# A trunk layer on one core: order of the products at each seam, x loads, first norm, last norm

## The chip, the core and the metric

The kernel runs on one core of a Trainium2 chip. TensorE (PE) multiplies, with its weight loads (PEld) beside it; VectorE (DVE), ScalarE (ACT) and GpSimd (POOL) work on tiles; SyncE (SP) and POOL issue the transfers. Every engine takes its instructions in the order in which they stand in its own queue, so one that waits holds up all behind it. The metric is the device time of one execution in microseconds. Before the change it was 1810.94 us, the median of 3 runs (1808.47 to 1815.28).

## What is computed

One decoder layer for 256 tokens of 2048 values in float32: half-step FFN, a mixer of two kinds of heads, half-step FFN, final norm.

```python
x = x + 0.5 * swiglu(rmsnorm(x, ffn1_norm), ffn1_w_gate, ffn1_w_up, ffn1_w_down)
h = rmsnorm(x, mix_norm)
a_q, a_k, a_v, m_q, m_k, m_v, m_o, m_i, m_f = split(h @ w_in)
x = x + concatenate([y_a, y_b]) @ w_out        # differential attention, mLSTM
x = x + 0.5 * swiglu(rmsnorm(x, ffn2_norm), ffn2_w_gate, ffn2_w_up, ffn2_w_down)
return rmsnorm(x, final_norm)
```

The hidden width is 5632, so the six FFN matrices, 46 MB each, make up most of what is read.

## The kernel before

**Three matmuls for one product.** Every float32 operand is split into a high and a low part: ACT casts the high part (`wh`, `xs`, `xt`; L115 or L110), DVE subtracts it from the source (`wl` and the like; L116 or L111). PE then makes high by high, high by low and low by high (L145, L146, L148), each 128x512. All matmuls run on such parts, so a weight tile always goes load, ACT, DVE, PE.

**Paired chunks.** Columns are done in chunks of 512, with two accumulators, one for each half of the tokens. `Paired` takes two column chunks (gate and up, or two chunks of a down projection) and, for the first `ns` pairs of row tiles, saves one product in eight by sums of blocks. Its `first()` loads a pair of both weights (`raw`, 2 x 512 KB), DVE forms `sums` (L376) and overwrites one block (L378), and after the splits PE makes P5 and P7 from the sums and then P1 and P6 from `raw`. Behind them the POOL queue adds one block of `raw` onto another by a transfer (L385). `combine()` stands at the seam to the next stage: ACT copies P1 to `u1` (L392), DVE adds P6 to it as `u2` (L393) and adds `u2` to P7 (L394), ACT copies that to `u3` (L395), and DVE forms the right chunk's accumulators (L396, L397). 44 such seams run. `second()` finishes the left chunk in P1 and P7: `bare(j)` with the blocks of `raw` that the POOL transfer has summed, `upper` for a third accumulator, and `plain` for the pairs that were not saved. `third()` finishes the right chunk; it is a stream that is woven into the next `first()`. There are six banks for accumulators and two (`ps_tr`) for transposes, and four `wh` and `wl` buffers.

**Stages.** FFN1 does its 11 hidden chunks in parts of 3, 3, 3 and 2. After each part come two paired down projections (c=0 and c=2); those of the first three parts have `ns`=3 and add their results into the residual `xres` through `part` (L286) and a POOL transfer (L287). Then come the mixer, `w_out` and FFN2 in the same way. A finished hidden chunk is transposed on PE (`hid_transposes`, L301, tile `hg`), a finished chunk of `xres` by `chunk_to_xt` (L248, tile `xg`); both are put on the list `pending`, from which `flush` takes them, and their splits and block sums (`xsum`, L278 to L280) run on ACT and DVE.

**Start and end.** `load_xt` loads the transposed x in 8 units of 256 KB (`xraw`, L553) among the first gate weights; `xres` (L566, 1 MB for each half of the tokens) is issued with a lower priority. `rstd1` squares `xres` in eight pieces (L235), and the row factor `rstd` is a power on POOL (L230), needed by the gate's Silu (`sg`, L314). At the end `store` does the last norm for one half of the tokens after the last column chunk.

**What sets the order.** A scheduler places each engine's instructions by priority: `tc.high_priority(offset=AHEAD)` moves work 400 steps forward (weight loads and splits), `soon()` 440 steps (`combine`, copies of transposes), the rest stands at its place in the program.

## Time and profile before

| | |
|---|---|
| Median of 3 runs | 1810.94 us |
| Profiled execution, and its span | 1805.68 us, 1803.9 us |
| DVE, ACT and POOL busy | 1571.9 us (87%), 1170.5 us (65%), 174.1 us (10%) |
| Transfers | 402.75 MB, mean 223 GB/s |
| Granted clock | 0.999 |

All times inside the execution count from the start of the span. A row of the timeline has the start, the length, the engine, the line, the operation with its tiles (out<-in) and, in brackets, how long the engine had stood idle before it and what released it. "SPq" is the moment at which SP issues a transfer, and not the transfer. PE's matmuls overlap, so a PE row's length is more than the step from one to the next.

### The profile page before, as it was taken

The numbers are of one execution on the slowest core, as the hardware profiler recorded it, in microseconds if no ns is written. First come the engines' busy times: TensorE is split into PE (matmuls) and PEld (weight loads), VectorE is DVE, ScalarE is ACT, GpSimd is POOL, SyncE is SP. The second block draws the span as 40 slices with busy tenths as digits, with TensorE's granted clock in tenths as the row PEclk, the third lists the DMA queues.
The fourth block names the chain that finished last, engine by engine and source line by source line (L and its number), as shares of the span: only waits on it lengthen the run. The fifth ranks groups of instructions, "written<-read, shape, count | busy, mean of one in ns | idle before, by whom it ended". The sixth has DMA issues, their size and how long they took to land.

```text
span 1803.9 us, 23316 instructions
## 1 busy us (share of the span) xinstructions
PE 1777.9 (99%) x8033; PEld 1461.1 (81%) x8033; DVE 1571.9 (87%) x1889; ACT 1170.5 (65%) x1523; POOL 174.1 (10%) x218
## 2 busy tenths in 40 slices
PE   9999999999999999999999999999999999999998
PEld 6788788888787887987888888788788878888886
DVE  6988889988998988797787988899889988998986
ACT  6666666666666666676565766666666666666664
POOL 0001100111002100000001000101100021002100
PEclk9999999999999999999999999999999999999999
DMA  8677887787778974676656666777887788678954
GB/s 339 216 216 231 226 253 222 241 242 229 218 240 246 271 234 126 214 227 184 190 185 210 182 190 180 218 232 228 230 243 234 239 239 246 210 241 249 267 188 152
DMA packets 125255, 402.75 MB, mean 223 GB/s; under 512 B 14160, under 2 KB 14160, under 8 KB 124880
## 3 DMA queue, kind: packets, MB, share of 16 engines
q1 hardware_dynamic: 96624, 349.28, 56.3%
q0 software_dynamic: 27216, 49.56, 16.2%
q10 hardware_dynamic: 1296, 2.42, 0.4%
q8 instruction: 63, 1.03, 0.2%
q14 instruction: 56, 0.46, 0.1%
HBM read 349.56 MB, written 2.10 MB: 195 GB/s over the span
## 4 chain that ended last, share of the span: by engine, by line
PE 85%; DMA 4%; DVE 3%; issue 2%; ACT 1%; POOL 1%; SPq 0%; POOLq 0%; DVEq 0%; ACTq 0%
PE acc L145 27%; PE acc L146 27%; PE acc L148 27%; DMA raw<-raw 3%; DVE wl L116 2%; PE tr L301 1%; ACT wh L115 0%; DMA raw<-in_wd_dram 0%; POOL xres L287 0%; PE sc L895 0%; POOL raw L385 0%; PE tr L248 0%; PE num L846 0%; DVE sums L376 0%; DVE acc L394 0%
## 5 line engine op out<-in xcount | busy, mean ns | idle before, releaser
L115 ACT CAST wh<-raw 128x1024 fp32r<-128x1024 f32 (+3 forms) x448 | 400.8, 907 | 245.1 <-PE acc L146 202.4
L145 PE MATMUL acc<-wh,xt 128*128 128x512 f32 (+2 forms) x1392 | 539.5, 389 | 1.4 <-ACT wh L115 0.8
L146 PE MATMUL acc<-wh,xt 128*128 128x512 f32 (+2 forms) x1392 | 538.4, 388 | 0.8 <-DVE xt L111 0.8
L116 DVE TENSOR_TENSOR wl<-raw,wh 128x1024 fp32r<-128x1024 f32 (+3 forms) x448 | 460.3, 1040 | 56.2 <-ACT wh L115 50.4
L116 DVE TENSOR_TENSOR wl<-rawp,wh 128x1024 fp32r<-128x1024 f32 (+1 forms) x358 | 431.7, 1209 | 69.3 <-ACT wh L115 57.6
L115 ACT CAST wh<-rawp 128x1024 fp32r<-128x1024 f32 (+1 forms) x358 | 372.7, 1043 | 154.4 <-PE acc L146 133.3
L145 PE MATMUL acc<-wh,xs 128*128 128x512 f32 (+2 forms) x1123 | 441.5, 396 | 10.3 <-ACT u L395 5.8
L146 PE MATMUL acc<-wh,xs 128*128 128x512 f32 (+2 forms) x1123 | 434.4, 389 | 0.5 <-DVE xs L111 0.5
L148 PE MATMUL acc<-wl,xt 128*128 128x512 f32 (+2 forms) x1392 | 388.1, 388 | 1.4 <-DVE wl L116 1.4
L148 PE MATMUL acc<-wl,xs 128*128 128x512 f32 (+2 forms) x1123 | 347.6, 387 | 0.1
L145 PEld LDWEIGHTS acc<-wh,xt 128*128 128x128 f32 x1392 | 261.2, 188 | 55.5 <-ACT xt L110 1.4
L146 PEld LDWEIGHTS acc<-wh,xt 128*128 128x128 f32 x1392 | 261.5, 188 | 54.1 <-DVE xt L111 1.6
L148 PEld LDWEIGHTS acc<-wl,xt 128*128 128x128 f32 x1392 | 260.0, 188 | 55.4 <-DVE wl L116 3.1
L145 PEld LDWEIGHTS acc<-wh,xs 128*128 128x128 f32 x1123 | 211.4, 188 | 62.8 <-ACT u L395 11.0
L385 POOL DMA_DIRECT2D raw<-raw x141 | 120.0, 851 | 1379.2 <-DVE wl L116 1137.2
L146 PEld LDWEIGHTS acc<-wh,xs 128*128 128x128 f32 x1123 | 211.6, 189 | 41.5 <-DVE xs L111 1.7
L148 PEld LDWEIGHTS acc<-wl,xs 128*128 128x128 f32 x1123 | 209.7, 188 | 43.6 <-DVE wl L116 1.0
L115 ACT CAST wh<-sums 128x1024 fp32r<-128x1024 f32 x141 | 148.6, 1054 | 113.6 <-PE acc L146 103.8
L376 DVE TENSOR_TENSOR sums<-raw 128x1024 f32<-128x1024 f32 x141 | 172.4, 1223 | 54.3 <-DMA raw<-in_wu_dram 28.3
L116 DVE TENSOR_TENSOR wl<-sums,wh 128x1024 fp32r<-128x1024 f32 x141 | 172.0, 1220 | 15.1 <-ACT wh L115 14.9
L378 DVE TENSOR_TENSOR raw<-sums,raw 128x512 f32<-128x512 f32 x141 | 96.5, 685 | 0.3
L287 POOL DMA_DIRECT2D xres<-part x48 | 45.5, 1169 | 96.0 <-ACT part L286 96.0
(191 smaller groups left out, 809.7 us busy)
## 6 DMA issues: line engine op xcount, KB each, us to landing
rawp<-in_wd_dram SPq DMA_DIRECT2D x96, 512.0 KB, 6.2
rawp<-in_wu_dram SPq DMA_DIRECT2D x94, 512.0 KB, 6.4
raw<-in_wg_dram SPq DMA_DIRECT2D x89, 512.0 KB, 7.0
rawp<-in_wg_dram SPq DMA_DIRECT2D x86, 512.0 KB, 5.3
raw<-in_wu_dram SPq DMA_DIRECT2D x82, 512.0 KB, 7.7
raw<-in_wd_dram SPq DMA_DIRECT2D x80, 512.0 KB, 6.4
raw<-raw POOLq DMA_DIRECT2D x141, 256.0 KB, 5.7
rawp<-in_win_dram SPq DMA_DIRECT2D x50, 512.0 KB, 4.6
```

The lines of the kernel that those rows point to most:

```text
L115: nc.scalar.copy(hi, src)
L116: nc.vector.tensor_tensor(out=lo, in0=src, in1=hi.bitcast(F32), op=ALU.subtract)
L145: nc.tensor.matmul(acc, lh, rh, start=first, stop=False, skip_group_check=on)
L146: nc.tensor.matmul(acc, ll, rh, start=False, stop=False, skip_group_check=on)
L148: nc.tensor.matmul(acc, lh, rl, start=False, stop=last, skip_group_check=on)
L287: nc.gpsimd.dma_start(xres[:, hb, c * CW:(c + 1) * CW], t, accum_op=ALU.add)
L301: nc.tensor.transpose(tr[:, i, hb * P:(hb + 1) * P], hs[hb][:, k * P:(k + 1) * P], ident)
L376: nc.vector.tensor_tensor(out=sums, in0=raw[:, 0:4:3, :], in1=raw[:, 2:3, :].to_broadcast([P, 2, CW]), op=ALU.add)
L378: nc.vector.tensor_tensor(out=raw[:, 2, :], in0=sums[:, 0, :], in1=raw[:, 3, :], op=ALU.add)
L385: nc.gpsimd.dma_start(raw[:, 2, :], raw[:, 1, :], accum_op=ALU.add)
```

## The change

At the last saved pair of each `first()` the order is now P1, P6, P7, P5, with the split of `raw` ahead of that of `sums`; the pairs before it keep P5, P7, P1, P6. `combine` works in one tile `u` in place of `u1` and `u2`. The transposes go on the list one by one (`run(j)`), and their splits have the priority of weight splits. The copies `sg` and `part` get `soon()`. The mixer's input gets three saved pairs, not four. At the start, x comes in two loads of 256 KB and three of 512 KB, the Silu table is loaded first, one block sum of x is made inside `load_xt`, and `rstd1` squares each half of the tokens in one instruction. Two small loads move from ACT's queue to POOL's. The last norm runs in two column halves of the last chunk, and the output leaves in pieces of 544 and 480 columns.

```diff
--- before.py
+++ after.py
...
+CUTS = ((0, 544, 0), (1088, 1568, 1), (544, 1088, 0), (1568, 2048, 1))
...
-    nc.scalar.copy(touch[:, 0:1], touch[:, 1:2])
+    nc.scalar.activation(touch[:, 0:1], touch[:, 1:2], AF.Silu)
...
     def chunk_to_xt(c, gbase, xp, ns):
-        for j in range(2 * c, 2 * c + 2):
+        def run(j):
             tr = ps_tr.tile([P, 2, S], F32, tag="tr", name=nm("tr"))
...
+            with tc.high_priority(offset=AHEAD):
+                if j < ns:
+                    sum_pair(xp, j, gained(tr, prm[:, gbase + 2 * j:gbase + 2 * j + 2]))
+                else:
+                    hi, lo = plain_pair(xp, j)
+                    for i in range(2):
+                        split_gain(tr[:, i, :], gbase + 2 * j + i, hi[:, i, :], lo[:, i, :])
+        pending.extend(functools.partial(run, j) for j in (2 * c, 2 * c + 1))
...
     def add_part(acc, hb, c):
...
         t = wk("part")
-        nc.scalar.activation(t, acc, AF.Copy, scale=0.5)
+        with soon():
+            nc.scalar.activation(t, acc, AF.Copy, scale=0.5)
         nc.gpsimd.dma_start(xres[:, hb, c * CW:(c + 1) * CW], t, accum_op=ALU.add)
...
     def hid_transposes(hs, hid, c, ns):
-        for j in range(2 * c, 2 * c + 2):
+        def run(j):
             tr = ps_tr.tile([P, 2, S], F32, tag="tr", name=nm("tr"))
...
                 act.copy(g, tr.rearrange("p a b -> p (a b)"))
-                sum_pair(hid, j, g.rearrange("p (a b) -> p a b", b=P))
+                with tc.high_priority(offset=AHEAD):
+                    sum_pair(hid, j, g.rearrange("p (a b) -> p a b", b=P))
             else:
-                split(tr, *plain_pair(hid, j))
+                with tc.high_priority(offset=AHEAD):
+                    split(tr, *plain_pair(hid, j))
+        pending.extend(functools.partial(run, j) for j in (2 * c, 2 * c + 1))
     def gate(src, r):
         s = wk("sg")
-        nc.scalar.activation(s, src, AF.Silu, scale=r)
+        with soon():
+            nc.scalar.activation(s, src, AF.Silu, scale=r)
         return s
...
                         load_pair(raw[:, 2 * i:2 * i + 2, :], w, self.k0 + 2 * j)
-                    f = pair_tiles(wsp, "w", [P, 2, CW])
                     sums = wrp.tile([P, 2, CW], F32, tag="rawp", name=nm("sums"))
...
                     nc.vector.tensor_tensor(out=raw[:, 2, :], in0=sums[:, 0, :], in1=raw[:, 3, :], op=ALU.add)
-                    e = pair_tiles(wsp, "w", [P, 2, CW])
-                    split(sums, *f)
-                    split(raw[:, 0:3:2, :], *e)
-                mms([self.job(self.p5, j, S1, f, 0, at, end), self.job(self.p7, j, S3, f, 1, at, end)])
-                mms([self.job(self.p1, j, A1, e, 0, at, end), self.job(self.p6, j, S2, e, 1, at, end)])
+                    split_of = {}
+                    for src in ("et" if end else "te"):
+                        split_of[src] = pair_tiles(wsp, "w", [P, 2, CW])
+                        split(sums if src == "t" else raw[:, 0:3:2, :], *split_of[src])
+                e, f = split_of["e"], split_of["t"]
+                p16 = [self.job(self.p1, j, A1, e, 0, at, end), self.job(self.p6, j, S2, e, 1, at, end)]
+                if end:
+                    mms(p16)
+                    mms([self.job(self.p7, j, S3, f, 1, at, end)])
+                    mms([self.job(self.p5, j, S1, f, 0, at, end)])
+                else:
+                    mms([self.job(self.p5, j, S1, f, 0, at, end), self.job(self.p7, j, S3, f, 1, at, end)])
+                    mms(p16)
                 with tc.high_priority(offset=AHEAD):
...
         def combine(self):
-            u1, u2, u3 = wk("u1"), wk("u2"), wk("u3")
+            u, u3 = wk("u"), wk("u3")
             p1, p5, p6, p7 = self.p1, self.p5, self.p6, self.p7
             with soon():
-                nc.scalar.copy(u1, p1)
-                nc.vector.tensor_tensor(out=u2, in0=p6, in1=u1, op=ALU.add)
-                nc.vector.tensor_tensor(out=p7, in0=p7, in1=u2, op=ALU.add)
+                nc.scalar.copy(u, p1)
+                nc.vector.tensor_tensor(out=u, in0=p6, in1=u, op=ALU.add)
+                nc.vector.tensor_tensor(out=p7, in0=p7, in1=u, op=ALU.add)
                 nc.scalar.copy(u3, p7)
                 nc.vector.tensor_tensor(out=p6, in0=p5, in1=u3, op=ALU.subtract)
-                nc.vector.tensor_tensor(out=p5, in0=p5, in1=u2, op=ALU.subtract)
+                nc.vector.tensor_tensor(out=p5, in0=p5, in1=u, op=ALU.subtract)
         def plain(self, w, k, accs, apart=False):
...
                         self.plain(self.wa, self.rest[i], (n11, n21), True)()
-                if i % 2 == 0:
-                    flush()
+                flush(0 if i % 2 else None)
                 aside(mid)
...
                     hs = [gated(au[hb], r[:, hb:hb + 1], sg[hb]) for hb in range(NT)]
-                pending.append(functools.partial(hid_transposes, hs, hid, c, ns))
+                hid_transposes(hs, hid, c, ns)
...
                     half(linear(xp, wg[0], KD, ahead=first[0], in_pieces=True))
-                    first[1]()
                     au = []
...
+    xraws = {}
     def load_xt(u):
-        k = u * UK
-        raw = slots.tile([P, UK, S], F32, tag="s", name=nm("xraw"))
+        k, i = u * UK, u % 2 * UK
         with tc.high_priority(offset=AHEAD):
-            nc.sync.dma_start(raw, xt[:, k:k + UK, :])
+            if i == 0:
+                xraws[u // 2] = slots.tile([P, 2 * UK, S], F32, tag="s", name=nm("xraw"))
+            both = xraws[u // 2]
+            raw = both[:, i:i + UK, :]
+            if u < 2:
+                nc.sync.dma_start(raw, xt[:, k:k + UK, :])
+            elif i == 0:
+                nc.sync.dma_start(both, xt[:, k:k + 2 * UK, :])
             if u < NP:
...
                 split_gain(raw[:, t, :], G_FFN1 + k + t, hi[:, t, :], lo[:, t, :])
+        if u == KD // UK - 1:
+            sum_xt()
         if u >= KD // UK - NT:
...
     def sum_xt():
...
         raw, j, hi, lo = gs.pop(0)
-        sums(gained(raw, prm[:, G_FFN1 + j * UK:G_FFN1 + j * UK + UK]), hi, lo)
+        with tc.high_priority(offset=AHEAD):
+            sums(gained(raw, prm[:, G_FFN1 + j * UK:G_FFN1 + j * UK + UK]), hi, lo)
...
     r1 = {}
...
     def rstd1():
         if not r1:
+            tot = small.tile([P, NT], F32, tag="tot", name=nm("tot"))
             for hb in range(NT):
-                for c in range(4):
-                    square_sum(xres[:, hb, c * CW:(c + 1) * CW], parts1[:, hb, c:c + 1])
-            r1[0] = finish_norm(parts1)
+                j = slots.tile([P, D], BF16, tag="s", name=nm("junk"))
+                nc.scalar.activation(j, xres[:, hb, :], AF.Square, accum_out=tot[:, hb:hb + 1])
+            r1[0] = rsq(tot, NT, float(D), "rstd")
         return r1[0]
...
     def finish1(c, accs):
         residual(accs, c, 0.5, parts2)
-        pending.append(functools.partial(chunk_to_xt, c, G_MIX, xp2, NP))
+        chunk_to_xt(c, G_MIX, xp2, NP_MIX)
...
-    nc.scalar.dma_start(bif, bias_if.partition_broadcast(P))
+    nc.gpsimd.dma_start(bif, bias_if.partition_broadcast(P))
...
-    nc.scalar.dma_start(lv, lamv.partition_broadcast(P))
+    nc.gpsimd.dma_start(lv, lamv.partition_broadcast(P))
...
     def finish_out(c, accs):
         residual(accs, c, 1.0, parts3)
-        pending.append(functools.partial(chunk_to_xt, c, G_FFN2, xp3, NP))
+        chunk_to_xt(c, G_FFN2, xp3, NP)
...
-    def store(hb):
-        tot = small.tile([P, 1], F32, tag="tot4", name=nm("tot"))
-        nc.vector.tensor_reduce(out=tot, in_=parts4[hb], axis=AX.X, op=ALU.add)
-        r = rsq(tot, 1, float(D), "rstd4")
-        for c in (1, 0, 3, 2):
-            xs = xres[:, hb, c * CW:(c + 1) * CW]
-            if c == 0 or c == 2:
-                nc.scalar.activation(xs, xs, AF.Copy, scale=r)
-            elif c == 1:
-                nc.vector.tensor_scalar(xs, xs, r, None, op0=ALU.mult)
+    def store(hb, acc):
+        h = CW // 2
+        xs = [xres[:, hb, 3 * CW + i * h:3 * CW + (i + 1) * h] for i in range(2)]
+        parts = small.tile([P, 2], F32, tag="tot4", name=nm("tot"))
+        v = small.tile([P, 1], F32, tag="v4", name=nm("v4"))
+        nc.vector.tensor_reduce(out=v, in_=parts4[hb][:, 0:3], axis=AX.X, op=ALU.add)
+        nc.vector.tensor_scalar(v, v, 1.0 / D, EPS, op0=ALU.mult, op1=ALU.add)
+        for i in range(2):
+            nc.vector.scalar_tensor_tensor(xs[i], acc[:, i * h:(i + 1) * h], 0.5, xs[i], op0=ALU.mult, op1=ALU.add)
+            square_sum(xs[i], parts[:, i:i + 1])
+        def times_gain(i):
+            nc.vector.tensor_tensor(out=xs[i], in0=xs[i], in1=fn[1][:, 1, i * h:(i + 1) * h], op=ALU.mult)
+        times_gain(0)
+        with tc.high_priority(offset=20):
+            for i in range(2):
+                nc.vector.scalar_tensor_tensor(v, parts[:, i:i + 1], 1.0 / D, v, op0=ALU.mult, op1=ALU.add)
+        times_gain(1)
+        r = small.tile([P, 1], F32, tag="rstd4", name=nm("rstd4"))
+        nc.gpsimd.tensor_tensor(out=r, in0=v, in1=mhalf[:, 0:1], op=ALU.pow)
+        for a, b, engine in CUTS:
+            y = xres[:, hb, a:b]
+            if engine:
+                nc.scalar.activation(y, y, AF.Copy, scale=r)
             else:
-                nc.vector.scalar_tensor_tensor(xs, xs, r, fn[1][:, 1, :], op0=ALU.mult, op1=ALU.mult)
-            (nc.sync if c % 2 else nc.scalar).dma_start(out[hb * P:(hb + 1) * P, c * CW:(c + 1) * CW], xs)
+                nc.vector.tensor_scalar(y, y, r, None, op0=ALU.mult)
+            (nc.scalar if engine else nc.sync).dma_start(out[hb * P:(hb + 1) * P, a:b], y)
     def finish2(c, accs):
...
         for hb in range(NT):
+            if c == 3:
+                store(hb, accs[hb])
+                continue
             xs = xres[:, hb, c * CW:(c + 1) * CW]
...
             square_sum(xs, parts4[hb][:, c:c + 1])
-            if c < 3:
-                nc.vector.tensor_tensor(out=xs, in0=xs, in1=fn[c // 2][:, c % 2, :], op=ALU.mult)
-            else:
-                store(hb)
+            nc.vector.tensor_tensor(out=xs, in0=xs, in1=fn[c // 2][:, c % 2, :], op=ALU.mult)
...
```

How this moves instructions is seen at three places. The first is the start, on SP, which issues x, the first gate weights (`raw`), up weights (`rawp`) and `xres`. Before:

```order
L128 DMA raw_301<-in_wg_dram 128x1024 x2
L553 DMA xraw_236<-in_xt_dram 128x512
L172 DMA rawp_373<-in_wu_dram 128x1024
L172 DMA rawp_391<-in_wu_dram 128x1024
L553 DMA xraw_243<-in_xt_dram 128x512
L172 DMA rawp_409<-in_wu_dram 128x1024
L566 DMA xres<-in_x_dram 128x2048
L553 DMA xraw_285<-in_xt_dram 128x512
L566 DMA xres<-in_x_dram 128x2048
L553 DMA xraw_293<-in_xt_dram 128x512
```

And of the change:

```order
L129 DMA raw_244<-in_wg_dram 128x1024 x2
L578 DMA xraw_232<-in_xt_dram 128x1024
L129 DMA raw_302<-in_wg_dram 128x1024 x2
L578 DMA xraw_279<-in_xt_dram 128x1024
L173 DMA rawp_352<-in_wu_dram 128x1024
L173 DMA rawp_370<-in_wu_dram 128x1024
L173 DMA rawp_388<-in_wu_dram 128x1024
L173 DMA rawp_406<-in_wu_dram 128x1024
L593 DMA xres<-in_x_dram 128x2048 x2
```

The up weights and `xres` now stand behind the last x load, where three of the first and both of the second stood ahead of it.

The second place is DVE at the seam of a c=2 down projection (third part of FFN1; the subtractions from `raw` are those of `bare` and `upper`). Before:

```order
L116 TENSOR_TENSOR wl_3241<-raw_3090,wh_3240 128x1024
L116 TENSOR_TENSOR wl_3253<-rawp_3250,wh_3252 128x1024
L116 TENSOR_TENSOR wl_3269<-raw_3135,wh_3268 128x1024
L393 TENSOR_TENSOR u_663_3226<-acc_3087,u_662_3225 128x512
L394 TENSOR_TENSOR acc_3088<-acc_3088,u_663_3226 128x512
L116 TENSOR_TENSOR wl_3279<-raw_3090,wh_3278 128x512
```

And of the change:

```order
L117 TENSOR_TENSOR wl_3211<-raw_3061,wh_3210 128x1024
L117 TENSOR_TENSOR wl_3223<-rawp_3220,wh_3222 128x1024
L412 TENSOR_TENSOR u_3196<-acc_3058,u_3196 128x512
L117 TENSOR_TENSOR wl_3239<-raw_3106,wh_3238 128x1024
L413 TENSOR_TENSOR acc_3059<-acc_3059,u_3196 128x512
L117 TENSOR_TENSOR wl_3249<-raw_3061,wh_3248 128x512
```

The addition into `u` has moved ahead of the second `bare` split; on ACT the copy of P1 stands ahead of that split's cast in the same way.

The third place is DVE between `w_out` and FFN2, from the sum of the squares (`tot`) to the input of `rstd` (`rsqv`). Before:

```order
L239 TENSOR_REDUCE tot_9956<-parts_8735 128x2
L116 TENSOR_TENSOR wl_9979<-raw_9970,wh_9978 128x1024
L376 TENSOR_TENSOR sums_10065<-raw_10060 128x1024
L116 TENSOR_TENSOR wl_10000<-rawp_9997,wh_9999 128x1024
L378 TENSOR_TENSOR raw_10060<-sums_10065,raw_10060 128x512
L376 TENSOR_TENSOR sums_10110<-raw_10105 128x1024
L116 TENSOR_TENSOR wl_10019<-sums_10020,wh_10018 128x1024
L116 TENSOR_TENSOR wl_10024<-raw_10015,wh_10023 128x1024
L378 TENSOR_TENSOR raw_10105<-sums_10110,raw_10105 128x512
L116 TENSOR_TENSOR wl_10045<-rawp_10042,wh_10044 128x1024
L228 TENSOR_SCALAR rsqv_9958<-tot_9956 128x2
```

And of the change, from the last residual addition (L298) on:

```order
L298 SCALAR_TENSOR_TENSOR xres<-acc_9092,xres 128x512
L117 TENSOR_TENSOR wl_9818<-rawp_9815,wh_9817 128x1024
L240 TENSOR_REDUCE tot_9901<-parts_8683 128x2
L229 TENSOR_SCALAR rsqv_9903<-tot_9901 128x2
L117 TENSOR_TENSOR wl_9834<-raw_9623,wh_9833 128x1024
L112 SCALAR_TENSOR_TENSOR xt_9778<-tr_9773,prm,xt_9778 128x256
L112 SCALAR_TENSOR_TENSOR xt_9788<-tr_9783,prm,xt_9788 128x256
L386 TENSOR_TENSOR sums_9918<-raw_9915 128x1024
```

`rsqv` now follows `tot` at once, where nine instructions of the first gate and up chunk stood between them, and both stand ahead of that chunk's first `sums`.

7 lines of the change are left out of this document (removed).

## Prediction

> **What bounds the kernel now.** I read the page first: PE is busy for 99% of the span, and the chain that ended last runs 85% on PE. Since busy PE rows overlap, I then read what PE waits for, and a stretch in which it waits for nothing.
>
> ```profile
> span 1803.9 us, 23316 instructions
> PE 1777.9 (99%) x8033; PEld 1461.1 (81%) x8033; DVE 1571.9 (87%) x1889; ACT 1170.5 (65%) x1523; POOL 174.1 (10%) x218
> ...
> PE 85%; DMA 4%; DVE 3%; issue 2%; ACT 1%; POOL 1%; SPq 0%; POOLq 0%; DVEq 0%; ACTq 0%
> ```
>
> ```profile
> PE acc L145 <- ACT u L395: 5.8, 7, 1.1
> PE acc L145 <- ACT wh L115: 2.4, 3, 1.3
> PE acc L145 <- ACT sg L314: 2.2, 5, 1.3
> PE tr L248 <- ACT xg L333: 1.7, 2, 1.0
> PE acc L148 <- DVE wl L116: 1.4, 3, 0.9
> ```
>
> ```profile
> 1054.18 0.39 PE L145 MATMUL acc<-wh,xt 128*128 128x512 f32 x1
> ...
> 1055.77 0.39 PE L146 MATMUL acc<-wh,xt 128*128 128x512 f32 x1
> ```
>
> ```profile
> 760.00:1060.00 300.00, 300.00 (x1423) 247.35 (x1422) 248.99 (x365) 200.49 (x317) 20.85 (x29) 1.00 0.64 197
> ```
>
> The work of PE does not change in this diff: eight matmuls between 1054.18 and 1055.77 start 0.227 us apart, before and after. What can go is PE's waits. The five wait rows hold 13.5 us in 20 waits (total, times, longest). A wait delays the issue by some 0.17 us more than its row says: idle counts from the modelled end of the matmul ahead, which lies 0.39 us behind its start, and not from the step of 0.227. That makes 17 us, and the waits on x below bring it to 19. The middle, 760 to 1060 us, has no wait. So each part is worth the waits in its own place, and all together no more than 19 us and what smaller ones add. The Trainium skill ("Perfetto Trace Analysis", section "Identifying the Most-Contended Engine") would have headroom judged by the busy share of the weight loads and not of the matmuls; by that, 81% leaves 19%, over 300 us. This trace disagrees: the stretch without waits reads 247.35 of 300, 82%, so 81% is nearly full, and I give a gain far beyond 20 us no chance.
>
> **The start: +2.0 us, from -1 to +4.**
>
> ```profile
> 15.17 0.50 PE L146 MATMUL acc<-wh,xs 128*128 128x512 f32 x1 [0.21 <-DVE xs L111]
> ...
> 18.48 0.50 PE L146 MATMUL acc<-wh,xs 128*128 128x512 f32 x1 [0.30 <-DVE xs L111]
> ...
> 21.69 0.73 PE L145 MATMUL acc<-wh,xt 128*128 128x512 f32 x2 [0.61 <-ACT xt L110]
> ...
> 22.93 0.50 PE L146 MATMUL acc<-wh,xt 128*128 128x512 f32 x1 [0.51 <-DVE xt L111]
> ```
>
> ```profile
> 19.55 0.33 SPq L553 DMA_DIRECT2D xraw<-in_xt_dram  x1
> ```
>
> ```profile
> L333 ACT ACTIVATE xg<-xraw,prm x8: 493/504/512, 44.2 to 53.4; 128x256 f32<-128x256 f32 x8
> ...
> DMA to landing us min/median/max: 3.2/8.5/10.8
> ```
>
> ```profile
> 24.00:32.00 8.00, 7.76 (x34) 5.88 (x32) 3.54 (x5) 4.30 (x7) 0.00 (x0) 1.00 1.01 406
> ```
>
> The transfers run full (share 1.01, 406 GB/s), so 512 KB take 1.29 us, in one load or in two. The last x load is issued at 19.55 and lands up to 10.8 us later, at 30.4. Ahead of it stand 2 MB of `xres` (5.2 us) and three up weights (3.9 us), all of which now stand behind. So it lands near 30.4-9.1 = 21.3 us, and the four waits on x (1.63 us, with 0.17 each 2.3) should go. Against that, ACT now makes the first block sum's two copies of x (0.50 each) ahead of the first weight cast; half of their 1.0 us lies in time spent waiting for that weight, so I take 0.4 off.
>
> ```profile
> 39.16 0.63 ACT L235 ACTIVATE junk<-xres 128x512 bf16<-128x512 f32 x1
> ...
> 41.79 1.28 ACT L314 ACT_TABLE_LOAD   x1
> ...
> 43.09 1.27 ACT L314 ACTIVATE sg<-acc,rstd 128x512 f32<-128x512 f32 x2
> ...
> 46.13 0.50 PE L145 MATMUL acc<-wh,xt 128*128 128x512 f32 x1 [0.79 <-ACT wh L115]
> ```
>
> PE's wait at 46.13 (0.79, so 0.95) is for ACT. On ACT's queue the table load of 1.28 us goes, and eight squares become two. One of 2048 columns is not in the trace; it takes more than the 0.63 of 512 columns and at most four times that, 2.5 us. I take 2.2, nearer the four: it is the same work with one fixed start. Little time is saved by it, but each holds ACT for 2.2 us where a weight cast came between the small ones, and `xres` lands later. I count a new wait of 0.8 us in place of the old 0.95. So 2.3-0.4+0.95-0.8 = 2.0 us. If the x waits stay by half and the new wait is 2.5, it is -1; if none comes and 25 to 65 us lose theirs, +4. The Trainium skill ("ScalarE: Activation LUTs", section "What ACT_TABLE_LOAD costs") adds a drain of 1.38 us to a load of 1.28 us. The load agrees, but Silu begins at 43.09, 0.02 us behind its end; with a drain the start would gain up to 1.4 us more, and this trace shows none to save.
>
> **Six down seams: +4.0 us, from 0 to +6.** These are the c=2 seams of parts with three pairs; they hold nearly all of the first wait row (5.8 us). One of them:
>
> ```profile
> 560.33 1.05 ACT L115 CAST wh<-raw 128x1024 fp32r<-128x1024 f32 x1 [2.01 <-DMA raw<-raw]
> ...
> 561.42 1.23 DVE L116 TENSOR_TENSOR wl<-raw,wh 128x1024 fp32r<-128x1024 f32 x1 [1.83 <-ACT wh L115]
> ...
> 562.56 0.68 DVE L393 TENSOR_TENSOR u<-acc,u 128x512 f32<-128x512 f32 x1
> ```
>
> ```profile
> 564.65 0.49 PE L145 MATMUL acc<-wh,xs 128*128 128x512 f32 x1 [1.07 <-ACT u L395]
> ```
>
> The chain is POOL transfer, cast, `wl`, `u2`, the addition to P7, `u3`, PE. P1 and P6 now end six matmuls (1.36 us) earlier, and the order puts the copy of P1 ahead of the cast and its addition ahead of that `wl`. DVE's 1.83 us idle there cover the 0.68. So `u2` leaves the chain: 0.68 a seam, six times, 4.0 us. Late next are the same transfer, cast and `wl`, for which PE still waits some 0.4 us. If the cover is gone (P1 not done when ACT comes to its copy, and the cast queued behind), the gain is 0; if the waits go wholly, 6.
>
> **Hidden splits: +2.2 us, from 0 to +3.2.**
>
> ```profile
> L376 DVE TENSOR_TENSOR sums<-raw 128x1024 f32<-128x1024 f32 x141 | 172.4, 1223 | 54.3 <-DMA raw<-in_wu_dram 28.3
> L116 DVE TENSOR_TENSOR wl<-sums,wh 128x1024 fp32r<-128x1024 f32 x141 | 172.0, 1220 | 15.1 <-ACT wh L115 14.9
> L378 DVE TENSOR_TENSOR raw<-sums,raw 128x512 f32<-128x512 f32 x141 | 96.5, 685 | 0.3
> ```
>
> ```profile
> 288.90 0.50 PE L145 MATMUL acc<-wh,xs 128*128 128x512 f32 x1 [0.21 <-ACT sg L314]
> ```
>
> ```profile
> 475.82 1.20 PE L148 MATMUL acc<-wl,xt 128*128 128x512 f32 x4 [0.91 <-DVE wl L116]
> ```
>
> ```profile
> 1374.30 0.50 PE L145 MATMUL acc<-wh,xs 128*128 128x512 f32 x1 [0.22 <-ACT sg L314]
> ```
>
> ```profile
> 477.23 0.69 DVE L116 TENSOR_TENSOR xs<-hg,xs 128x512 fp32r<-128x512 f32 x1
> ```
>
> In `first()` a pair and its stream unit cost DVE 1.22+0.69+3x1.22 = 5.6 us, PE 24 steps, 5.4. DVE has nothing to spare, and the sums and splits of a transposed pair land there: two splits of 0.69 and some 1 us of sums, 2.4 us. With high priority they move into `second()`, where a step has 2.5 `wl`, 3.1 us, beside 21 matmuls, 4.8. Seven waits between 288.90 and 1374.30 are of this kind, on `wl` or on a late `sg`, 3.2 us with the lag. I take two thirds, since the priority also puts this work ahead of weight splits.
>
> **Start of the mixer: +1.0 us, from 0 to +2.5.**
>
> ```profile
> 696.00 0.66 PE L248 MATMUL tr<-ident,xres 128*128 128x128 f32 x4 [1.03 <-ACT xg L333]
> ...
> 698.33 0.50 PE L145 MATMUL acc<-wh,xs 128*128 128x512 f32 x1 [0.34 <-ACT u L392]
> ```
>
> Sixteen transposes stand in a row with two banks for them, and three waits (the wait row's 1.7 and this 0.34, 2.5 us with the lag) follow. Put on the list one by one, the fourth group comes 20 matmuls later and the copy of P1 earlier; the third group still waits, about 1.2.
>
> **Seam of `w_out`: -1.2 us, from -2.5 to 0.** The same list works against PE at the c=2 seam near 1055 us, in the stretch without waits. After the change twelve transposes stand together ahead of the first `bare`, and ACT has a square, two `xg` and two casts ahead of the copy of P1. The third group waits as at 696.00: 1.03 and the lag.
>
> **Start of FFN2: +2.2 us, from 0 to +2.6.**
>
> ```profile
> 1127.76 0.15 DVE L239 TENSOR_REDUCE tot<-parts 128x2 f32<-128x8 f32 x1
> ...
> 1138.09 0.16 DVE L228 TENSOR_SCALAR rsqv<-tot 128x2 f32<-128x2 f32 x1
> ```
>
> ```profile
> 1138.23 1.20 PE L148 MATMUL acc<-wl,xt 128*128 128x512 f32 x4 [0.30 <-DVE wl L116]
> ...
> 1140.72 0.50 PE L145 MATMUL acc<-wh,xs 128*128 128x512 f32 x1 [1.30 <-ACT sg L314]
> ```
>
> The input of the row factor lies 10 us in DVE's queue; the power and Silu follow it, and PE stands 1.30 us. With `rsqv` behind `tot`, that is over before the gate's products end: 1.5 us, and 0.7 for most of the 0.5 at 1138.23 and a like wait at 1127.9, where splits of x come earlier. The new wait of `tot` for its squares holds weight splits behind it on DVE for less than their 0.63.
>
> **The end: 0, from -0.5 to +0.5.** The same bytes are normalised in halves, one square becomes two of half the width, and the output still leaves behind the power.
>
> **Sum:** 2.0+4.0+2.2+1.0-1.2+2.2 = 10.2 us. The profiled execution took 1805.68 us, 1.8 more than its span, and would take 1795.5. It ran 5.3 us under the median of the runs shown, so on their scale the forecast is 1810.94-10.2 = 1800.7, told as **1801 us**. About 0.5%, 9 us, is what a measurement of this kernel tells from no change; that line is at 1801.9, close to the forecast.
>
> **Rivals.** *The chains are only rearranged* (0.20): the seams keep their chain because the copy of P1 comes off ACT no sooner, and DVE pays for the hidden splits elsewhere. For it: DVE is busy for 87%. Against: its 1.83 us idle at the seam. The 4.0 and 2.2 go: 1807. *The start gives nothing* (0.12): long squares hold ACT and all casts behind them, and at 46.13 ACT is late already. Then -1 in place of 2.0: 1804. *The x loads were hidden and no wait listed goes* (0.05): 1811. *Slower* (0.10): the priority turns on `second()`. Both pairs of a hidden chunk are flushed together, 4.8 us of DVE work ahead of `wl`, against 1.7 us of slack in a step; the other 3.1 must be covered by splits that have run ahead into the four buffers. In `first()` the same work cost at most 1.1 us at one place, which speaks against it. If the lead is 1 us short at each of 22 hidden chunks, 22 us are lost and 10.2 won: 1823. It decides from 0.9 us a chunk on. My forecast has 0.53, of which 0.45 lie under the line; of the first two rivals 0.08 lie there too, since their other parts can end higher. So faster 0.53, same 0.37, slower 0.10.
>
> **Range.** All upper ends together are 18.8 us, 1792; with nothing gained it is 1811. So 1791 to 1811.
>
> **What will show it.** Start right: no PE wait on x from 15 to 26 us; wrong: a wait on `wh` near 43 over 1.5 us. Seams: waits on `u3` near 0.4 us at six places; wrong: unchanged. Splits: no wait on `wl` near 476; wrong: new ones in `second()`. FFN2: no wait on `sg` near 1140. `w_out`: a new wait on `xg` of about 1 us near 1055. The whole forecast is wrong if new waits appear at many of the 44 seams.

## The result, and the profile after

The changed kernel takes 1799.18 us (median of 6 runs, 1796.86 to 1801.86) beside 1811.0 for the kernel before (6 runs, 1807.9 to 1815.77): ratio 0.9931, 95% interval 0.9913 to 0.9948. Run again among the experiments it took 1800.89 us (8 runs) beside 1808.34, ratio 0.9961 (0.9948 to 0.9973). So the gain is 7 to 12 us; by the second comparison it lies under the 9 us that the prediction took as the line to no change. The profiled execution of the changed kernel took 1801.86, the slowest of its six, where that of the kernel before (1805.68) was below all six runs beside it; the two traces differ by 3.8 us only, and are compared by place.

The page of the changed kernel, its span and the busy times:

```profile
span 1800.1 us, 23366 instructions
...
PE 1775.1 (99%) x8033; PEld 1462.9 (81%) x8033; DVE 1566.0 (87%) x1895; ACT 1164.6 (65%) x1512; POOL 177.7 (10%) x220
```

What PE waits for in it (total, times, longest):

```profile
PE acc L146 <- ACT sg L325: 7.0, 5, 1.9
PE acc L146 <- ACT u L414: 3.7, 6, 1.2
...
PE acc L146 <- ACT xs L111: 1.0, 1, 1.0
PE tr L250 <- ACT xg L344: 1.0, 1, 1.0
PE acc L146 <- ACT u L411: 0.8, 2, 0.4
PE acc L146 <- ACT wh L116: 0.7, 1, 0.7
```

Waits on `u3` (L395 before, L414 now) fell from 5.8 to 3.7 us, those on `wl` are gone, and those on `sg` rose from 2.2 to 7.0. Since both kernels make as many matmuls of each shape, 8033 in all, their traces can be laid side by side by the number of the matmul. For each place I summed how much longer each step from matmul to matmul was than the median step of its shape in that trace; that includes slow steps behind a wait. "Before" has one profile, the changed kernel two:

| issue lost, us | before | changed | changed, again | forecast of the gain |
|---|---|---|---|---|
| start, to 160 us | 7.74 | 3.64 | 6.13 | 2.0 |
| six c=2 seams | 8.44 | 3.48 | 2.70 | 4.0 |
| six seams behind them (c=0 and others) | 1.08 | 3.87 | 2.08 | none |
| five hidden chunks (near 280, 470, 1175, 1365, 1555 us) | 4.73 | 10.44 | 9.28 | 2.2 |
| start of the mixer | 3.11 | 2.29 | 2.29 | 1.0 |
| `w_out`, 1040 to 1100 us | 0.53 | 1.57 | 1.59 | -1.2 |
| start of FFN2 | 3.29 | 0.04 | 0.04 | 2.2 |
| last matmul to the end | 8.76 | 9.08 | 9.15 | 0 |

**The start** of the changed kernel: the last x load on SP, the two PE waits that the timeline has from 6 to 50 us, and the first of the two squares.

```profile
11.68 0.33 SPq L578 DMA_DIRECT2D xraw<-in_xt_dram  x1
```

```profile
6.72 0.73 PE L146 MATMUL acc<-wh,xs 128*128 128x512 f32 x2 [1.05 <-ACT xs L111]
8.83 0.74 PE L146 MATMUL acc<-wh,xs 128*128 128x512 f32 x1 [0.67 <-ACT wh L116]
```

```profile
32.11 1.91 ACT L608 ACTIVATE junk<-xres 128x2048 bf16<-128x2048 f32 x1
```

The last x load is issued 7.9 us earlier than before; it lands at 21.88, where I worked out 21.3. All waits on x between 15 and 26 us are gone. A square of 2048 columns takes 1.91 us, not the 2.2 taken, and no wait on `wh` follows near 46 us.

**A c=2 seam**, the one at 564.65 us before, now:

```profile
559.10 2.09 ACT L116 CAST wh<-raw 128x1024 fp32r<-128x1024 f32 x3 [1.93 <-DMA raw<-raw]
560.18 1.23 DVE L117 TENSOR_TENSOR wl<-raw,wh 128x1024 fp32r<-128x1024 f32 x1 [1.63 <-ACT wh L116]
561.32 0.69 DVE L413 TENSOR_TENSOR acc<-acc,u 128x512 f32<-128x512 f32 x1
...
562.05 0.59 ACT L414 COPY u<-acc 128x512 f32<-128x512 f32 x1 [0.86 <-DVE acc L413]
...
562.68 0.50 PE L146 MATMUL acc<-wh,xs 128*128 128x512 f32 x1 [1.20 <-ACT u L414]
```

The chain is the forecast one: POOL transfer, cast, `wl`, the addition to P7, `u3`, PE, with the addition into `u` out of it. From the cast's start to PE it is 3.58 us, before 4.32, so 0.74 shorter (0.68 forecast). PE still waits 1.20 at this seam (and 0.81 at the one at 180.75; at the other four it has no wait): it ran dry 2.1 us earlier than before (561.48 against 563.58), and the transfer let the cast start only 1.2 us earlier.

**A hidden chunk, the wait on `sg` near 278 us.** DVE, SP, ACT and PE of the changed kernel:

```profile
260.96 0.69 DVE L117 TENSOR_TENSOR xs<-hg,xs 128x512 fp32r<-128x512 f32 x1
261.57 0.42 DVE L283 TENSOR_TENSOR xsum<-hg 128x256 f32<-128x256 f32 x1
...
265.47 1.22 DVE L117 TENSOR_TENSOR wl<-raw,wh 128x1024 fp32r<-128x1024 f32 x1
266.61 0.69 DVE L117 TENSOR_TENSOR xs<-xsum,xs 128x512 fp32r<-128x512 f32 x1
267.21 1.29 DVE L117 TENSOR_TENSOR wl<-raw,wh 128x512 fp32r<-128x512 f32 x2
```

```profile
258.04 0.52 SPq L173 DMA_DIRECT2D raw<-in_wu_dram  x1
267.97 0.33 SPq L173 DMA_DIRECT2D raw<-in_wg_dram  x1
...
268.82 0.99 SPq L173 DMA_DIRECT2D rawp<-in_wu_dram  x2
```

```profile
276.66 1.04 ACT L116 CAST wh<-rawp 128x1024 fp32r<-128x1024 f32 x1 [2.63 <-DMA rawp<-in_wu_dram]
277.61 0.68 ACT L325 ACTIVATE sg<-acc,rstd 128x512 f32<-128x512 f32 x1
...
278.34 0.62 PE L146 MATMUL acc<-wh,xs 128*128 128x512 f32 x1 [1.87 <-ACT sg L325]
```

And SP of the kernel before, at the same chunk:

```profile
262.66 0.51 SPq L172 DMA_DIRECT2D raw<-in_wu_dram  x1
263.22 0.80 SPq L172 DMA_DIRECT2D rawp<-in_wu_dram  x1
270.80 0.33 SPq L172 DMA_DIRECT2D raw<-in_wg_dram  x1
271.17 0.44 SPq L172 DMA_DIRECT2D rawp<-in_wu_dram  x1
```

What SP waits for in the changed kernel from 255 to 280 us (total, times, longest):

```profile
SPq L173 <- DVE wl L117: 21.2, 3, 9.3
```

Before, the stream's weight `rawp` was issued 0.56 us behind the last `raw`, ahead of a pause of SP of 6.8 us (264.02 to 270.80), and landed at 271.54. Now DVE does the sums and splits of two hidden pairs between 260.96 and 267.3, among the `wl` whose end frees load buffers; SP issues nothing from 258.56 to 267.97, 9.4 us, waiting for a `wl`. And `rawp` has changed its place in SP's queue: it stands behind the pause and the next two `raw`, 10.8 us behind the `raw` that it followed before, and lands at 276.58. Of these 10.2 us more, 2.6 are the longer pause and the rest the new place. The cast of this load waits 2.63 us on ACT, and `sg`, which would free a bank, stands behind the cast.

**`w_out` and FFN2** in the changed kernel: the waits that the twelve transposes bring, and the Silu that PE waited for at 1140.72 before.

```profile
1057.50 1.30 PE L250 MATMUL tr<-ident,xres 128*128 128x128 f32 x7 [0.24 <-DVE xres L298]
1059.13 0.50 PE L146 MATMUL acc<-wh,xs 128*128 128x512 f32 x1 [0.34 <-ACT u L411]
```

```profile
1128.04 1.27 ACT L325 ACTIVATE sg<-acc,rstd 128x512 f32<-128x512 f32 x2
```

### The profile page after: what moved, and what is told of

The parts are those of the page before. It is cut to its first block, busy times and chain, and to the rows that moved or that the text cites. A ratio compares the mean times of both kernels' runs of the same rounds, so it can differ in the third digit from the quotient of the medians.

```text
span 1800.1 us, 23366 instructions
## 1 busy us (share of the span) xinstructions
PE 1775.1 (99%) x8033; PEld 1462.9 (81%) x8033; DVE 1566.0 (87%) x1895; ACT 1164.6 (65%) x1512; POOL 177.7 (10%) x220
## 3 DMA queue, kind: packets, MB, share of 16 engines
q8 instruction: 63, 1.03, 0.2%
## 4 chain that ended last, share of the span: by engine, by line
PE 88%; DMA 4%; DVE 4%; issue 2%; ACT 2%; SPq 0%; POOL 0%; POOLq 0%; ACTq 0%; DVEq 0%
PE acc L146 28%; PE acc L149 28%; PE acc L147 28%; DMA rawp<-in_wu_dram 2%; DVE wl L117 2%; DMA raw<-raw 1%; PE tr L307 1%; ACT wh L116 1%; DMA raw<-in_wd_dram 0%; DVE xs L117 0%; DMA raw<-in_wg_dram 0%; PE num L874 0%; SPq L173 0%; DVE acc L413 0%; PE tr L250 0%
## 5 line engine op out<-in xcount | busy, mean ns | idle before, releaser
L146 PE MATMUL acc<-wh,xt 128*128 128x512 f32 (+3 forms) x1444 | 558.9, 388 | 0.0
L147 PE MATMUL acc<-wh,xt 128*128 128x512 f32 (+3 forms) x1444 | 557.1, 387 | 0.0
L146 PE MATMUL acc<-wh,xs 128*128 128x512 f32 (+2 forms) x1071 | 422.5, 396 | 13.4 <-ACT sg L325 7.0
L147 PE MATMUL acc<-wh,xs 128*128 128x512 f32 (+2 forms) x1071 | 414.9, 388 | 0.0
L149 PE MATMUL acc<-wl,xt 128*128 128x512 f32 (+3 forms) x1444 | 401.2, 387 | 0.0
L149 PE MATMUL acc<-wl,xs 128*128 128x512 f32 (+2 forms) x1071 | 339.7, 389 | 0.1
L146 PEld LDWEIGHTS acc<-wh,xt 128*128 128x128 f32 x1444 | 271.5, 188 | 55.0 <-ACT xt L116 0.6
L147 PEld LDWEIGHTS acc<-wh,xt 128*128 128x128 f32 x1444 | 271.6, 188 | 54.4
L149 PEld LDWEIGHTS acc<-wl,xt 128*128 128x128 f32 x1444 | 269.7, 188 | 54.6 <-DVE wl L117 0.3
L404 POOL DMA_DIRECT2D raw<-raw x141 | 124.2, 881 | 1349.0 <-DVE wl L117 1191.5
L146 PEld LDWEIGHTS acc<-wh,xs 128*128 128x128 f32 x1071 | 201.2, 188 | 61.6 <-ACT sg L325 9.1
L149 PEld LDWEIGHTS acc<-wl,xs 128*128 128x128 f32 x1071 | 200.6, 189 | 43.0 <-DVE wl L117 1.7
L147 PEld LDWEIGHTS acc<-wh,xs 128*128 128x128 f32 x1071 | 201.5, 188 | 38.6 <-DVE xs L112 0.4
```

What stands on the lines that cost most here:

```text
L146: nc.tensor.matmul(acc, lh, rh, start=first, stop=False, skip_group_check=on)
L147: nc.tensor.matmul(acc, ll, rh, start=False, stop=False, skip_group_check=on)
L149: nc.tensor.matmul(acc, lh, rl, start=False, stop=last, skip_group_check=on)
L404: nc.gpsimd.dma_start(raw[:, 2, :], raw[:, 1, :], accum_op=ALU.add)
```

## The experiments

Each ran beside the kernel before on one chip. "Lost" is the issue lost by place, worked out as in the table above.

**1. The gate's Silu at plain priority.** The first theory laid the five waits on `sg` to `soon()` on it.

```diff
 def gate(src, r):
     s = wk("sg")
-    with soon():
-        nc.scalar.activation(s, src, AF.Silu, scale=r)
+    nc.scalar.activation(s, src, AF.Silu, scale=r)
```

> The changed kernel, with the gate's Silu (sg) back at its plain priority; all else as changed. Theory 1: the five new waits on sg (7.0 us in all in the changed kernel's profile, and a granted clock down to 0.86 to 0.90 behind one of them) come from soon() on sg, because PE is then ordered to take the next chunk's P1 and P6 at once, into banks that sg has yet to empty. Without it the waits on sg fall to 2.5 us or less, and the time to 1793 to 1796, ratio about 0.990. Theory 2: they come from the transposed splits that now stand ahead of the weight splits on DVE, so that load buffers come free late and loads land late; then PE waits at the same five places for wh or wl instead, and the time stays at 1799 within 2 us.

Measured: 1800.15 us, ratio 0.9957 (0.9944 to 0.9971). Its PE waits:

```profile
PE acc L146 <- ACT wh L116: 5.4, 7, 1.4
PE acc L146 <- ACT sg L324: 4.1, 5, 0.8
```

The waits on `sg` fell by 2.9 us, and those on `wh` rose from 0.7 to 5.4, 2.0 of it at the start. The five chunks lose 10.76, as much as with `soon()`. Theory 1 falls: the order of `sg` only decides which instruction shows the late load.

**2. The seam order alone.** The kernel before with the changed `first()` and `combine()`, and nothing else of the change.

```diff
-mms([self.job(self.p5, ...), self.job(self.p7, ...)])
-mms([self.job(self.p1, ...), self.job(self.p6, ...)])
+if end:
+    mms(p16)
+    mms([self.job(self.p7, j, S3, f, 1, at, end)])
+    mms([self.job(self.p5, j, S1, f, 0, at, end)])
...
-u1, u2, u3 = wk("u1"), wk("u2"), wk("u3")
+u, u3 = wk("u"), wk("u3")
```

> The kernel before, with only the last pair's order P1, P6, P7, P5 and the one tile u. Theory 1 (the addition u2 leaves the chain): the six c=2 seams lose 2.0 to 2.8 us in place of 6.4, that is 4 us won; the c=0 seams get new waits on u3 of some 0.5 us at four places, 2.4 us lost; sum 1809, ratio 0.998 to 0.999. Rival (chains only rearranged): the six seams as before, 1811 and more, ratio 1.000 to 1.002.

Measured: 1802.96 us, ratio 0.997 (0.996 to 0.9979): better than expected, though its profile is its slowest run (1806.84). The c=2 seams lose 3.69 in place of 8.44, as the forecast mechanism has it. The rival falls. The five chunks lose 8.27 in place of 4.73, which I had not expected: the order alone also moves loads there (in this trace the stream's weight lands at 279.03 near the first chunk, before at 276.08).

**3. The start alone.** The kernel before with the changed x loads, table, block sum and squares.

```diff
-nc.scalar.copy(touch[:, 0:1], touch[:, 1:2])
+nc.scalar.activation(touch[:, 0:1], touch[:, 1:2], AF.Silu)
...
-        nc.sync.dma_start(raw, xt[:, k:k + UK, :])
+        if u < 2:
+            nc.sync.dma_start(raw, xt[:, k:k + UK, :])
+        elif i == 0:
+            nc.sync.dma_start(both, xt[:, k:k + 2 * UK, :])
...
-            for c in range(4):
-                square_sum(xres[:, hb, c * CW:(c + 1) * CW], parts1[:, hb, c:c + 1])
+            nc.scalar.activation(j, xres[:, hb, :], AF.Square, accum_out=tot[:, hb:hb + 1])
```

> The kernel before, with only the new start: x loads, Silu table first, block sum in load_xt, squares over token halves. Theory 1 (the last x load lands 9 us earlier, so PE is fed): matmul number 500 runs 4.4 us earlier, as in the changed kernel, and the time is 1806.6, ratio 0.9975. Rival (squares and copies of x hold up the casts as soon as other edits are gone): 2 us or less by matmul 500, 1809 or more.

Measured: 1806.64 us, ratio 0.9989 (0.9977 to 1.0002). Up to 160 us it loses 5.61, of which 2.27 are one wait on `u3` at 61 us, at the first gate and up seam. Matmul 500 runs at 121.13 us, before at 124.14: 3.0 us earlier, between the 4.4 of theory 1 and the 2 of the rival. The interval of the time reaches 1, so the runs alone don't show a gain.

**4. The lists and their priority alone.** `chunk_to_xt` and `hid_transposes` as changed; `sg` and `part` at plain priority.

```diff
-pending.append(functools.partial(hid_transposes, hs, hid, c, ns))
+hid_transposes(hs, hid, c, ns)
...
-pending.append(functools.partial(chunk_to_xt, c, G_MIX, xp2, NP))
+chunk_to_xt(c, G_MIX, xp2, NP_MIX)
```

> The kernel before, with only the transposes put on the list one by one, their splits at the weight splits' priority, and three saved pairs for the mixer; sg and part stay at plain priority. Theory 1: FFN2's start gains 3 us, the mixer's 0.8, w_out's seam loses 1.2, and there are no waits on sg of over 0.5 us: 1808, ratio 0.9985. Theory 2 (these splits alone hold up the loads): waits of 1 to 2 us at five hidden chunks (near 280, 472, 1175, 1365, 1555 us) and 1811 or more.

Measured: 1810.09 us, ratio 1.0009 (1.0 to 1.0018). Theory 2 holds in the main: two waits of 0.4 to 1.1 us (on `wh`, then on `sg`) at each of the five places, 9.28 us lost in place of 4.73, and 4.54 more some 42 us behind them, and no gain in time. FFN2's start loses 0.96 in place of 3.29, the mixer's 2.27, `w_out` 1.53: near what was expected. The c=2 seams lose 4.77, less than the 8.44 before, though their order is the old one. At the one near 1270 us ACT's cast waits 0.68 us for the POOL transfer, before 2.16: the transfer is there earlier; why is not shown.

**5. The changed kernel again**, as the measure for the next three.

> The changed kernel once more, as the measure for the three beside it on one chip. 1797 to 1800, ratio 0.993; waits on sg at five hidden chunks, of 1.2 us or more each, 7 us in all, as in its first profile; if these five are chance, they are at other places or gone.

Measured: 1800.89 us, ratio 0.9961. Five waits on `sg` at the same places, 7.4 us in all. They are not chance. The ratio expected was 0.993.

**6. Hidden splits at plain priority.** The changed kernel; single transposes on the list and `soon()` on `sg` stay.

```diff
 act.copy(g, tr.rearrange("p a b -> p (a b)"))
-with tc.high_priority(offset=AHEAD):
-    sum_pair(hid, j, g.rearrange("p (a b) -> p a b", b=P))
+sum_pair(hid, j, g.rearrange("p (a b) -> p a b", b=P))
...
-with tc.high_priority(offset=AHEAD):
-    split(tr, *plain_pair(hid, j))
+split(tr, *plain_pair(hid, j))
```

> The changed kernel, with the block sums and splits of the transposed hidden back at plain priority; the list of single transposes and soon() on sg stay. Theory A (these splits, now ahead of the weight splits on DVE, hold back the buffers that SP waits for, so a stream's weight lands late and ACT's cast waits with sg behind it): the five waits on sg fall under 0.5 us each, and the time to 1793 to 1795, ratio 0.990. Theory B (the single transposes on the list, or soon() on sg, order PE that way whatever the splits do): waits of over 1 us remain at the five places, and the time is within 2 us of the changed kernel's.

Measured: 1799.63 us, ratio 0.9955 (0.994 to 0.997). Its PE waits:

```profile
PE acc L146 <- ACT wh L116: 4.1, 8, 1.5
PE acc L146 <- ACT u L412: 3.3, 5, 1.8
```

All waits on `sg` at the five places are gone, as theory A says (one of 0.7 is new at 130.85), but smaller ones on `wh` and `wl` came and the five chunks still lose 7.79. The time is not 1793 to 1795: splits are one cause, and not the only one.

**7. The hidden transposes wholly as before**, both pairs of a chunk as one entry of the list, plain priority.

```diff
-hid_transposes(hs, hid, c, ns)
+pending.append(functools.partial(hid_transposes, hs, hid, c, ns))
```

> The changed kernel, with hid_transposes wholly as before (both pairs of a chunk as one entry on the list, plain priority); all else as changed. Theory A: as hidden_splits_plain, 1793 to 1795, with the old waits on wl (near 470 and 1366 us, 0.4 to 1.1 us) back. Theory B with the list as the cause: better than hidden_splits_plain by 3 us or more. If hidden transposes don't matter: as the changed kernel, 1799 within 2 us.

Measured: 1797.9 us, ratio 0.9947 (0.9931 to 0.9962); the five chunks lose 6.75. It is 3.0 us under the changed kernel beside it, though the intervals overlap. Neither theory's time came: it is above 1793 to 1795, and only 1.7 us under experiment 6.

**8. Lists, priority and `soon()`.** Experiment 4 with `soon()` on `sg` and `part`.

```diff
+with soon():
     nc.scalar.activation(s, src, AF.Silu, scale=r)
```

> The kernel before, with the lists and priority of lists_and_priority and soon() on sg and part besides. If soon() is what turns the lists from a loss into a gain: the five waits of 0.5 to 1.2 us on sg 42 us behind the first ones (near 325, 515, 1221, 1411 and 1600 us) go, 4 us better than lists_and_priority, 1805 to 1806, ratio 0.9975. If soon() makes the first five waits longer by as much: 1809 to 1811, ratio 1.000 to 1.001.

Measured: 1807.93 us, ratio 0.9998 (0.9988 to 1.0009), between the two branches. The waits 42 us behind the chunks go (4.54 to 0.70 lost); the five chunks stay at 8.82. So `soon()` is worth about 2 us to the lists (the intervals overlap), and is not their trouble.

**9. The changed kernel with the old start**, the diff of experiment 3 undone.

> The changed kernel with the start as before (eight x loads, plain table first, block sums and eight squares where they stood). In five profiles with the new start the issue loses 3.6 to 6.1 us up to 160 us, in four with the old one 7.7 to 10.7. If the start is worth that difference, 4 to 5 us, this loses 8 us or more up to 160 us and has a ratio near 0.998 where the changed kernel had 0.996. If it is worth the 2 us of start_alone or less: 0.997 or below.

Measured: 1803.58 us, ratio 0.9967 (0.9955 to 0.998); it loses 9.27 to 160 us. The profile says that the start is worth 4 to 5 us. By the ratio, 0.9967 against 0.9961 for the changed kernel, it is worth 1; the intervals allow both.

**10. The new order without gate and up pairs.** Experiment 7, where the last pair is turned only outside of the gate and up pairs.

```diff
-if end:
+if turned:
...
-chain.run(Paired(xp, wg[done + c], wu[done + c], KD, np_), half, end)
+chain.run(Paired(xp, wg[done + c], wu[done + c], KD, np_, turn=False), half, end)
```

> The kernel hidden_as_before, with the last pair's new order kept for the down projections, w_out and the mixer, and the old order for gate and up pairs. If the new order of gate and up pairs is what makes a stream's weight land later at the five hidden chunks (their loss was 8.3 us with the order alone and 4.7 us before), they lose 5 us or less here in place of 6.75, the c=2 seams stay under 5 us, and the ratio is 0.9935, 1796 us. If the order there is harmless: as hidden_as_before, 0.9947.

Measured: 1801.44 us, ratio 0.9952 (0.9939 to 0.9966). The five chunks lose 2.86, less than before the change, as expected. But the time is not the 1796 expected. The c=2 seams lose 6.9 where under 5 was expected (1.77 of it is one wait at 565.08), FFN2's start loses 1, and the first gate and up seam now waits:

```profile
64.51 0.57 PE L146 MATMUL acc<-wh,xs 128*128 128x512 f32 x1 [3.65 <-ACT u L412]
```

**11. The same with the hidden splits as changed:** the diff of experiment 10 on the changed kernel.

> The changed kernel, with the last pair's old order for gate and up pairs alone. If splits and order each hold up the loads: the five hidden chunks lose 7 to 8 us in place of 9.3 to 10.4, ratio 0.9945 to 0.995. If the splits' priority decides alone there: 9 us or more, ratio 0.996.

Measured: 1803.73 us, ratio 0.9968 (0.9957 to 0.998); the five chunks lose 8.94. It was 9 or more that was expected if the splits decide alone, and that is nearly so. It too waits at the first gate and up seam (3.16 us at 63.70). With the splits ahead, the old order of gate and up pairs doesn't help: either edit alone is enough to hold up the loads.

SP's queue shows how. With experiment 12 there are fourteen profiles, and at all five chunks each of them has one of three orders:

| hidden splits; gate and up order | profiles | SP's queue at the five chunks | lost there, us |
|---|---|---|---|
| plain; old | before, 3, 10, 12 | one `rawp` ahead of SP's pause, the next right behind the first `raw` after it | 2.7 to 4.7 |
| plain; new | 2, 6, 7 | one `rawp` ahead of the pause, the next behind two `raw` | 6.8 to 8.3 |
| ahead; old or new | changed kernel, 1, 4, 5, 8, 9, 11 | none ahead of the pause, two behind it and two `raw` | 8.6 to 10.8 |

The pause is about 2 us longer in the last group. Why the scheduler places `rawp` so is not shown.

**12. The order only where it pays.** Experiment 10, with the last pair turned also at the first gate and up pair of each FFN.

```diff
-KD, np_, turn=False)
+KD, np_, turn=done + c == (first is not None))
```

> As down_seams_only, with the new order also at the first gate and up pair of each FFN, where down_seams_only got waits of 3.8 us (64.5 us, on u3) and 0.8 us (1134 us). If both waits are there because the old chain through u2 is longer at these two seams, they fall to under 0.6 us together, the five hidden chunks stay at 3 to 5 us, and the time is 1796 to 1798, ratio 0.993 to 0.9945, at least 5 us less issue lost to waits than in the changed kernel's second profile is not expected, 2 us is. If the new order moves the loads at these chunks too: 1799 to 1801 and waits at later hidden chunks.

Measured: **1794.0 us** (5 runs, 1793.4 to 1795.12), ratio **0.9911** (0.9893 to 0.9929). Its waits, and SP at the chunk of 278 us:

```profile
PE acc L146 <- ACT u L412: 3.2, 5, 1.3
PE acc L149 <- DVE wl L117: 1.6, 3, 1.0
```

```profile
257.88 0.54 SPq L173 DMA_DIRECT2D raw<-in_wu_dram  x1
258.48 0.71 SPq L173 DMA_DIRECT2D rawp<-in_wu_dram  x1
```

`rawp` follows the last `raw` by 0.60 us again, and no wait on `sg` is left. It loses 4.82 us to 160 us, 4.34 at the c=2 seams, 2.65 at the five chunks and 0.03 at FFN2's start. That is 2 us under the best time expected. It is the best version run, though it did not run beside the changed kernel, and its interval overlaps the first one of that kernel (0.9913 to 0.9948).

## Why the prediction was right, step by step

The time, 1799.18, is 1.8 us from the forecast of 1801, and the gain of 7 to 12 us is of the size of the 10.2 forecast. In part that is luck. The term for the hidden splits had the wrong sign, the seams behind the c=2 seams were left out, the start and FFN2 gave more than forecast, and in that comparison the kernel before ran slower than beside the experiments.

- **Six down seams, +4.0:** the chain is right, and the size nearly. It is 0.74 us shorter, and the six places lose 8.44 before, 3.48 and 2.70 now. The order alone gives as much as was forecast (3.69 left). But waits near 0.4 us were forecast at six places, and they are 0.81 and 1.20 at two and none at four (in the second profile 1.35 at one): the time at which the POOL transfer lands decides too, and it also moves with the lists (4.77 left with these alone). How the gain divides between the two is open. Left out of the forecast were the seams behind them. DVE and PE of the changed kernel at one:

```profile
212.24 1.22 DVE L117 TENSOR_TENSOR wl<-raw,wh 128x1024 fp32r<-128x1024 f32 x1
...
213.37 0.69 DVE L413 TENSOR_TENSOR acc<-acc,u 128x512 f32<-128x512 f32 x1
...
214.74 0.50 PE L146 MATMUL acc<-wh,xs 128*128 128x512 f32 x1 [0.37 <-ACT u L414]
```

  The addition to P7 now stands behind a `wl` on DVE, and PE waits for `u3`; 1.0 to 2.8 us go back at these seams.
- **Start, +2.0:** right in mechanism, too small. Five profiles with the old start lose 7.7 to 10.7 us to 160 us, mean 9.6; seven with the new one, whatever else they change, 3.6 to 6.1, mean 5.0 (experiments 10 and 11 left out, for their wait of over 3 us at 64 us). So the term is 4.6. The profile of before had the least loss of its five. Of the two deductions, the new wait behind long squares (0.8) was a step 0.3 us late at 44.08; the one for the copies of x was not measured apart. By the ratios of experiments 3 and 9 the term is smaller, 2 and 1 us; which is right stays open.
- **Hidden splits, +2.2:** the step that failed. "With high priority they move into `second()`", where DVE has 1.7 us of slack in a step: they moved, and the five places lose 4.6 to 5.7 us more. The prediction counted the slack on DVE against PE alone. It left out SP: its loads wait for the buffers that `wl` frees, and with the new priority the stream's load stands behind such a wait and not ahead of it. The late load's cast then stands ahead of `sg` on ACT. That is the mechanism of the slower rival (priority in `second()`), at 5 of 22 hidden chunks and through loads and not through the lead of splits. Experiments 4 and 6 to 12 show it; experiment 2 shows that the new order of gate and up pairs also moves a load by itself. The waits to be won were also fewer than counted: the trace of before has six of them there and not seven, 2.0 us, 3.0 with the lag.
- **Mixer, +1.0, and `w_out`, -1.2:** 0.8 and -1.0, right in size. The one wait on `xg` left in the mixer is 1.0 us, the third group's, as forecast. At `w_out` the wait on `xg` that was forecast did not come: PE waits for `xres` at 1057.50 (0.24) and for the copy of P1 at 1059.13 (0.34), and is slowed among the transposes between. That the size fits is luck.
- **FFN2, +2.2:** 3.25, all waits there gone. With the lists alone 0.96 us stay.
- **End, 0:** -0.3 to -0.4.

With the start at 4.6 the terms by place sum to 4 and 7 us for the two profiles (4.6+5.3-1.9-5.1+0.8-1.0+3.25-0.35 = 5.6 for their mean), where 10.2 was forecast. That lies within the interval of the second comparison (7.4 us between medians, 5 to 9 by the ratios), and falls 6 us short of the first (11.8), where the kernel before ran 2.0 to 2.7 us above its medians beside the experiments. Why it did is open. The edits run alone point the same way: the order, the start and the lists with `soon()` (experiments 2, 3 and 8) save 0.0030, 0.0011 and 0.0002 of the time, 8 us together.

## What to carry to other kernels

A split that is moved ahead on a busy engine can be paid for by the loads whose buffers that engine frees: look at what SP issues, in what order and when, and not only at the engine's own slack. An order that shortens a chain belongs where the chain ends last; put everywhere, it moved loads at places that had nothing to win. With it taken back there, and the hidden splits too, the gain was 15 us in place of 7 to 12. Two programs with the same matmuls can be compared by the matmul's number, place by place, and this tells more than totals when executions scatter by some microseconds.

## What the runs showed of the hardware

One wait of 1.87 us, at 278.34 in the changed kernel's first profile, was followed by a lower granted clock. The windows view there (PE, PEld, DVE, ACT, POOL busy, then the clock):

```profile
280.00:285.00 5.00, 5.00 (x19) 4.02 (x18) 4.29 (x5) 2.30 (x4) 0.86 (x1) 0.80 0.98 243
```

Eight matmuls of 128x512 came 0.427 us apart in place of 0.227, so the wait cost about 3.5 us in all. In the second profile a wait of the same length near 280 us was followed by a clock of 1.00. Behind the first 20 us the fourteen profiles have six single waits of 1.75 to 1.9 us: two were followed by eight such steps (the other at 565.08 in experiment 10), four were not, and neither was one of 2.11 in experiment 3. Both waits over 3 us were (experiments 10 and 11, near 64 us). So were two waits of 1.03 and 0.68 close together at the start of the mixer in experiments 2 and 3, and not in the kernel before. The Trainium skill ("TensorE: Matmul & The Clock Gate", section "HAM oscillation — how this bites in real kernels") warns of idle gaps of over about 3.4 us; here slow steps also followed two single waits of under 1.9. What sets these apart from the others is not shown.
